# Four of six modulation groups of two layers made on VectorE, and fewer weight splits on GpSimd

## The chip, the core and the metric

The kernel runs on one core of a Trainium2 chip, as one program launched once. The metric is the device time of one execution in microseconds. TensorE multiplies matrices, VectorE and ScalarE do elementwise work, GpSimd does some more of it, and SyncE issues the DMAs. Each engine takes its own instructions in order and waits on semaphores for the others.

## The reference

Two blocks of two layers each run one after the other on `x` and a context, 256 tokens of 1024 features each. The first block's layers have a mixer of attention, Fourier and Hyena heads; the second's have a DeltaNet (layer 0) and a gated linear attention (layer 1). All four layers end in a feed-forward network (FFN). Each layer is steered by six vectors of 1024, made from a conditioning vector:

```
m = silu(c) @ w_mod + b_mod                        # 1024 -> 6 x 1024; c for x, c_ctx for the context
sh1, sc1, g1, sh2, sc2, g2 = split(m, 6)
x = x + g1 * mixer(rms_norm(x) * (1 + sc1) + sh1)
x = x + g2 * (relu(h @ w1) ** 2 @ w2),  h = rms_norm(x) * (1 + sc2) + sh2
```

In each block's second layer the context gives only keys and values, so it needs `sh1` and `sc1` alone: of groups 2 to 5 only the row of `c` is used there.

The DeltaNet has 8 heads of two value halves; each walks through four chunks of 128 tokens in both directions, its outputs are normalised per token and value half, multiplied by silu(z) (z is a projection of the layer's input, the gate), and multiplied by `w_out`.

## The kernel before

Activations lie feature by feature: a tile has 128 features in its partitions and the 512 tokens of both streams (`x` 0 to 255, context 256 to 511) in its columns. Every large matrix product is done in three passes on a reduced fp32 format. `weight` loads 512 KB of weights (`wr`), ScalarE rounds them to the high part `wh` (L307), and VectorE or GpSimd subtracts to get the low part `wl` (L308); this subtraction is called a split below. `mm3` issues the passes wh x rh, wh x rl, wl x rh (L316 to L318). For one tile of 128 output features and 1024 inputs that is 24 matmuls. GpSimd does the split where `pool=True` is passed (the first four weights of each FFN, two or so weights ahead of each next stage, some of the last mixer) and, by `pool_lo`, for the whole DeltaNet.

An FFN (`ffn`, `mlp`, `tail`) goes through four quarters. In each, the first matrix gives eight hidden tiles (24 matmuls each; then ScalarE's relu, VectorE's square at L610, ScalarE's L294 and VectorE's L295 for the two parts of it), and the second gives eight output tiles, added to `xs` at L659. FFN1 is that of the first block's layer 0, FFN2 that of the second block's layer 0; both have both streams, so n is 512.

The modulation vectors of all but the first layer's early groups are made in the background. `modulation` returns a list of steps, each a load of a few rows of 128 inputs (`wm`) and a piece of work. On TensorE (L394) the piece is 32 matmuls for four rows, which multiply silu(c) of both streams (`cvs`, 32 columns, two used) by 256 columns of weights, in four column strips of the array. The last piece of a group of 1024 outputs is followed, one step later, by `columns`: ScalarE's copy `ev`, four small matmuls (L405) that turn rows into columns, and the addition of the bias on VectorE (L406). `slot` is called after each tile of an FFN and starts a step each `every` slots; `quota` bounds the loads of a stage. The list runs in order: layer 1 of block 1, then both layers of block 2. The steps of block 1's layer 1 and part of block 2's fall into FFN1, later ones into FFN2; the tile `mod` of a layer is named `moda`, `modb` in the trace, and TensorE's output tile for it `pmd`.

The DeltaNet (`deltanet`) runs its heads in turn: `merge` and `steps` are long chains of small matmuls and VectorE operations, and between heads stand large products (`project`, `gates`, `write_out`) that fill TensorE meanwhile. `scale` normalises the outputs `ot` (the tiny operations are in `rsqrt`, L436 and L437), `readout` transposes them by eight matmuls (L452) and multiplies by the gates. For the last head nothing is left to project, so the generator `late` cuts the second gate and the output product of head 6 into 24 parts of three matmuls, which `between` puts into head 7's chains (16 of them at fixed places) while the rest follows after the last step. Then come `readout`, head 7's output product for stream `x` and then for the context, and behind each the norm for FFN2. SyncE's queue carries weights, `wm` loads and the DeltaNet's small transfers (`TT<-dout`) in program order.

Of the kernel before, what the change touches and what calls it, by code (L numbers as in the profile page):

```python
# [18 lines left out]
P = 128  # L19
# [15 lines left out]
def _moving(w):  # L35
    return _c(w.reshape(8, P, 6, 1024).transpose(2, 0, 1, 3))

# [92 lines left out]
def host_arrays(i):  # L130
# [5 lines left out]
    a["cv2"] = _c(np.stack([i["c_2"][0], i["c_ctx_2"]], 0).reshape(2, 8, P).transpose(2, 1, 0))  # L136
    for l in range(2):
# [67 lines left out]
class Net:  # L205
# [91 lines left out]
    def weight(self, src, into=None, pool=False, ahead=False):  # L297
# [22 lines left out]
    def lin(self, src, rhs, n0, n1, w=None, pool=False):  # L320
        w = w or self.weight(src, pool=pool)
        ps = self.mm_ps()
        self.mm3(ps[:, : n1 - n0], w, rhs, n0, n1)
        return ps[:, : n1 - n0]
# [42 lines left out]
    def modulation(self, wname, bname, cname, tag, batch=4, early=0):  # L367
# [47 lines left out]
        return mod, [s for cc in range(6) for s in steps(cc)]  # L415
# [103 lines left out]
    def follow(self, f, xs, S, gs, mod, shch, tag, win=None):  # L519
        f.update(h=self.rows16(), ws=None)  # L520

        def then(sv, y=None):
            if win and not f["ws"]:
                f["ws"] = [self.weight(w, pool=True, ahead=True) for w in win]
# [28 lines left out]
    def ffn(self, xs, g, w1, w2, mod, tag, streams, ys=None, h=None, quota=0, every=1, S=None, scales=None, before=None, then=None):  # L553
        one = len(streams) == 1
        with ExitStack() as st:
            self.pools(st, dict(n=(8, 256), h=3, acc=(4, 256), sq=(4, 256), rs=(1, 258)), dict(a=2, md=1, mm=5), 12 if one else 18, "a", quota)
# [4 lines left out]
            ws = [self.weight(self.a[w1][m], pool=True) for m in range(4)]  # L561
            self.background(1 if every == 2 else 0)
            self.load_ahead()
            self.every, self.slots = every, 0
# [5 lines left out]
            self.mlp(xs, h, ws, w1, w2, mod, 5, streams, S, scales or {"xc"[v]: 1.0 for (_, _, v) in streams}, before, then, nS)  # L570
# [4 lines left out]
    def mlp(self, xs, h, ws, w1, w2, mod, gch, streams, S, scales, before, then, nS):  # L575
        nc = self.nc
        n = 256 * len(streams)
        for s in range(4):
# [3 lines left out]
            for m in range(0, 8, 2):  # L582
# [13 lines left out]
                elif s == 0 and m == 0:  # L596
                    first = self.lins(ws[:4], h, streams)
# [73 lines left out]
    def pools(self, st, sb, ps, nr, pm, quota=0, pool_lo=False, nwm=2, wide=4, low=()):  # L671
        self.n += 1
        self.pool_lo = pool_lo
# [37 lines left out]
    def slot(self):  # L711
        self.slots += 1
        if self.slots % self.every == 0:
# [354 lines left out]
    def deltanet(self, xs, mod, h, ws, first):  # L1068
# [119 lines left out]
        def late(zs, og):  # L1188
            def use(ps):
                zs.append(ap.tile([P, 512], F32, tag="vf", bufs=2, name="z"))  # L1190
                nc.scalar.activation(zs[1], ps, AF.Silu)

            yield from self.lin_parts(lambda: self.weight(win[48]), h, 512, use)
# [124 lines left out]
        def merge(hd, c, parts):  # L1318
# [30 lines left out]
        def steps(hd, c, parts):  # L1349
# [4 lines left out]
            for step in range(4):  # L1354
                Sn = ap.tile([P, 512], F32, tag="S", bufs=2, name="S") if step < 3 else None
                for d in range(2):
# [31 lines left out]
                    self.between(parts, i.ins, 2 if step == 3 else 1)  # L1388
# [13 lines left out]
                S = Sn  # L1402
            return ot

        def scale(c, ot):
            ss = sp.tile([P, 4, 2], F32, tag="ss", name="ss")
            jk = junk()
            for ch in range(4):
                for v in range(2):
                    nc.scalar.activation(jk, ot[ch // 2][:, 256 * (ch % 2) + P * v : 256 * (ch % 2) + P * v + P], AF.Square,  # L1410
                                         accum_out=ss[:, ch, v : v + 1])
            nc.vector.scalar_tensor_tensor(ss, ss, 1.0 / 128, c["aq"].unsqueeze(2).to_broadcast([P, 4, 2]), ALU.mult, ALU.add)
            so = self.rsqrt(ss.rearrange("p c v -> p (c v)"), [P, 8], "o")
            for p in range(2):
                o = ot[p].rearrange("p (c i) -> p c i", i=P)
                nc.vector.tensor_tensor(o, o, so[:, 4 * p : 4 * p + 4].unsqueeze(2).to_broadcast([P, 4, P]), ALU.mult)
# [11 lines left out]
        def write_out(hd, og, S=None, then=None):  # L1428
            ws = [self.weight(a["dwout"][hd, mq]) for mq in range(2)]
            for sv in st if S else [(0, 512, 0)]:  # L1430
                for m in range(8):
                    c = slice(P * (m % 4), P * (m % 4) + P)
                    wh, wl = ws[m // 4]
                    ps = self.mm_ps()[:, : sv[1] - sv[0]]
                    self.mm3(ps, (wh[:, :, c], wl[:, :, c]), og, sv[0], sv[1])
                    if S:
                        self.finish(xs, m, ps, mod, 2, sv, S, dict(x=1.0, c=1.0))
                    else:
                        for s2 in st:
                            self.finish(xs, m, ps[:, s2[0] : s2[1]], mod, 2, s2, None, None)  # L1440
                if then:
                    then(sv)
# [5 lines left out]
        og, parts = None, iter(())  # L1448
        for hd in range(8):
            if hd == 7:  # L1450
                parts = late(zs, og)
            merge(hd, c, parts)
            ot = steps(hd, c, parts)
            if hd < 7:
                nxt = prepare(hd + 1, *proj)
            if 0 < hd < 7:
                write_out(hd - 1, og)
            if hd < 7:
                tokens(nxt)
# [4 lines left out]
            elif hd == 6:  # L1464
                zn = [gate(7, 0)]
            else:
                for part in parts:
                    part()
            with self.tc.issue_after(self.mark.ins):
                og = readout(ot, zs)  # L1470
            if hd < 6:
                zs = gates(hd + 1)
            elif hd == 6:
                zs = zn
            if hd < 7:
                c = nxt
# [4 lines left out]
        write_out(7, og, S, f["then"])  # L1481
# [4 lines left out]
    def gla(self, xs, mod, h, ws):  # L1486
# [46 lines left out]
        w3 = self.weight(win[2], [vtile().rearrange("p b n -> p (b n)").rearrange("p (k m) -> p k m", k=8).bitcast(F32R) for _ in range(2)], pool=True)  # L1533
# [5 lines left out]
        for m in range(4):  # L1539
            ps = self.lin(win[1 + m], h, 0, 512, w3 if m == 1 else None, True) if m else ps1  # L1540
# [6 lines left out]
        for m in range(4):  # L1547
            ps = self.lin(win[5 + m], h, 0, 256, None, m<3)
# [7 lines left out]
        def values(hd):  # L1556
            w = [self.weight(a["gwv"][hd, kh], pool=False) for kh in range(2)]
# [15 lines left out]
        def gate(hd):  # L1573
            zs = []
            for m in range(2):
                ps = self.lin(win[9 + 2 * hd + m], h, 0, 256, None, False)
# [146 lines left out]
    def run(self):  # L1723
# [8 lines left out]
        if not skip:  # L1732
            fng = None
            y = None
            for l in range(2):
                with ExitStack() as st:
# [5 lines left out]
                    self.pools(st, sb, ps, 7 if l else 10, "t", nwm=1, wide=3, low=("K", "V", "q", "PT", "E"))  # L1742
                    self.first_consts(st)
                    if l == 0:
# [4 lines left out]
                        mods = [self.modulation(f"wmod_{j}", f"bmod_{j}", "cv", f"a{j}", 4 if j else 3, 0 if j else 2) for j in range(2)]  # L1749
# [29 lines left out]
                        def early():  # L1779
                            self.background(2)  # L1780
                            ws = [self.weight(a["win_0"][m], pool=False) for m in (8, 9)]
                            self.background(5)
                            self.early = False
                            mods2.extend(self.modulation(f"amod_{j}", f"abmod_{j}", "cv2", f"b{j}") for j in range(2))
# [137 lines left out]
```

## Time and profile before

| what | value |
|---|---|
| time of three runs | 2652.54, 2655.13, 2656.1 us; median 2655.13 |
| the profiled execution | 2648.67 us |
| its span (first to last instruction) | 2646.9 us |
| mean granted TensorE clock | 0.977 of full speed |
| TensorE, VectorE, ScalarE, GpSimd busy | 95%, 62%, 43%, 14% of the span |

The span is the profiled execution without 1.8 us around it. A busy share is a mean over all stages, so what one stage is limited by is read from the windows of that stage. FFN1 lies between 328 and 694 us of the span, the DeltaNet's last head between about 1747 and 1853, FFN2 between 1866 and 2226. An instruction in the timeline has its start and its duration; the bracket behind it holds the idle time of its engine just before and what ended it.

### The profile page before, as it was taken

The numbers are of one execution on the slowest core, as the hardware profiler recorded it, in microseconds if no ns is written. First come the engines' busy times: TensorE is split into PE (matmuls) and PEld (weight loads), VectorE is DVE, ScalarE is ACT, GpSimd is POOL, SyncE is SP. The second block draws the span as 40 slices with busy tenths as digits, with TensorE's granted clock in tenths as the row PEclk, the third lists the DMA queues.
The fourth block names the chain that finished last, engine by engine and source line by source line (L and its number), as shares of the span: only waits on it lengthen the run. The fifth ranks groups of instructions, "written<-read, shape, count | busy, mean of one in ns | idle before, by whom it ended". The sixth has DMA issues, their size and how long they took to land. (4 is left out here: it accounts for less than half of the span.)

```text
span 2646.9 us, 40579 instructions
## 1 busy us (share of the span) xinstructions
PE 2503.5 (95%) x15740; PEld 2108.8 (80%) x15740; DVE 1648.9 (62%) x3449; ACT 1133.1 (43%) x2161; POOL 370.3 (14%) x268
## 2 busy tenths in 40 slices
PE   7999999999999999988999999977999999899999
PEld 4866877778886999867778877866877888698899
DVE  5555443333567777887877887767533435677676
ACT  3344333232355545663545444534422324564453
POOL 0000200000100100332333323312000001420100
PEclk8999999999999999999999999988999999999999
DMA  7334566663241466222122211211554522222554
GB/s 266 120 117 147 176 254 236 242 236 117 77 141 52 160 194 197 80 66 53 34 61 65 71 39 52 65 35 56 204 179 160 182 88 71 79 93 73 172 184 154
DMA packets 147105, 334.09 MB, mean 126 GB/s; under 512 B 57134, under 2 KB 68512, under 8 KB 146912
## 3 DMA queue, kind: packets, MB, share of 16 engines
q1 hardware_dynamic: 146656, 331.43, 38.6%
q8 instruction: 124, 2.03, 0.3%
q14 instruction: 69, 0.57, 0.1%
q0 software_dynamic: 256, 0.07, 0.0%
HBM read 327.78 MB, written 3.67 MB: 125 GB/s over the span
## 5 line engine op out<-in xcount | busy, mean ns | idle before, releaser
L307 ACT CAST wh<-wr 128x1024 fp32r<-128x1024 f32 (+1 forms) x421 | 426.1, 1016 | 700.2 <-PE pmm L317 511.4
L318 PE MATMUL pmm<-h,wl 128*128 128x512 f32 (+2 forms) x1800 | 624.6, 347 | 16.3 <-DVE wl L308 8.8
L316 PE MATMUL pmm<-h,wh 128*128 128x512 f32 (+2 forms) x1800 | 628.8, 349 | 6.9 <-ACT E L829 1.9
L317 PE MATMUL pmm<-h,wh 128*128 128x512 f32 (+2 forms) x1800 | 621.3, 345 | 0.0
L308 DVE TENSOR_TENSOR wl<-wr,wh 128x1024 fp32r<-128x1024 f32 (+1 forms) x333 | 392.3, 1180 | 288.8 <-ACT wh L307 282.3
L318 PE MATMUL pmm<-r,wl 128*128 128x256 f32 (+1 forms) x1312 | 444.3, 339 | 5.6 <-DVE wl L308 5.5
L316 PE MATMUL pmm<-r,wh 128*128 128x256 f32 (+1 forms) x1312 | 444.9, 340 | 4.5 <-DVE q L989 1.6
L317 PE MATMUL pmm<-r,wh 128*128 128x256 f32 (+1 forms) x1312 | 444.2, 339 | 0.1
L308 POOL TENSOR_TENSOR wl<-wr,wh 128x1024 fp32r<-128x1024 f32 x88 | 216.5, 2465 | 1383.1 <-ACT wh L307 724.4
L318 PEld LDWEIGHTS pmm<-h,wl 128*128 128x128 f32 x1800 | 346.6, 193 | 59.7 <-DVE wl L308 10.2
L316 PEld LDWEIGHTS pmm<-h,wh 128*128 128x128 f32 x1800 | 346.3, 192 | 53.0 <-issue 7.2
L317 PEld LDWEIGHTS pmm<-h,wh 128*128 128x128 f32 x1800 | 346.7, 193 | 37.1 <-issue 0.8
L316 PEld LDWEIGHTS pmm<-r,wh 128*128 128x128 f32 x1312 | 248.4, 190 | 38.7 <-issue 8.9
L318 PEld LDWEIGHTS pmm<-r,wl 128*128 128x128 f32 x1312 | 248.8, 190 | 32.0 <-DVE wl L308 7.0
L317 PEld LDWEIGHTS pmm<-r,wh 128*128 128x128 f32 x1312 | 249.1, 190 | 23.2 <-issue 1.7
L659 DVE SCALAR_TENSOR_TENSOR xs<-pmm,modb,xs 128x256 f32<-128x256 f32 x232 | 106.6, 477 | 133.0 <-PE pmm L318 133.0
L659 DVE SCALAR_TENSOR_TENSOR xs<-pmm,moda,xs 128x256 f32<-128x256 f32 x120 | 54.4, 480 | 146.7 <-PE pmm L318 146.5
L294 ACT CAST r<-h 128x256 fp32r<-128x256 f32 (+1 forms) x128 | 65.5, 513 | 126.8 <-DVE h L610 67.2
L295 DVE TENSOR_TENSOR r<-h,r 128x256 fp32r<-128x256 f32 (+1 forms) x128 | 72.9, 570 | 44.1 <-ACT r L294 40.7
L394 PE MATMUL pmd<-wm,cvs 128*32 128x256 f32 x1408 | 87.2, 382 | 0.0
L1371 ACT COPY e<-pa 128x256 f32<-128x256 f32 x64 | 23.8, 371 | 128.5 <-PE pa L1369 128.0
L394 PEld LDWEIGHTS pmd<-wm,cvs 128*32 128x32 f32 x1408 | 41.1, 109 | 40.1 <-issue 13.4
(484 smaller groups left out, 3834.7 us busy)
## 6 DMA issues: line engine op xcount, KB each, us to landing
wr<-w SPq DMA_DIRECT2D x128, 512.0 KB
wr<-f SPq DMA_DIRECT2D x128, 512.0 KB
wm<-amod SPq DMA_DIRECT2D x24, 2048.0 KB
wr<-dwin SPq DMA_DIRECT2D x49, 512.0 KB
wm<-wmod SPq DMA_DIRECT2D x12, 2048.0 KB
wr<-win SPq DMA_DIRECT2D x28, 512.0 KB
wm<-wmod SPq DMA_DIRECT2D x8, 1536.0 KB
wr<-gwin SPq DMA_DIRECT2D x17, 512.0 KB
```

Of the source, the lines that this page charges most:

```text
L294: self.nc.scalar.copy(hi, src)
L295: self.nc.vector.tensor_tensor(lo, src, hi.bitcast(F32), ALU.subtract)
L307: self.nc.scalar.copy(hi, raw)
L308: (self.nc.gpsimd if pool or self.pool_lo else self.nc.vector).tensor_tensor(lo, raw, hi.bitcast(F32), ALU.subtract)
L316: mm(ps, wh[:, k, :], rh[:, n0:n1], start=k == 0, stop=False)
L317: mm(ps, wh[:, k, :], rl[:, n0:n1], start=False, stop=False)
L318: self.mark = mm(ps, wl[:, k, :], rh[:, n0:n1], start=False, stop=k == last)
L394: self.last = nc.tensor.matmul(ps[32 * c : 32 * c + 32, :256], cs[:, k + i, :], raw[:, i, 256 * c : 256 * c + 256], start=k + i == 0, stop ...
L659: self.nc.vector.scalar_tensor_tensor(x, ps, mod[:, 8 * gch + m, v : v + 1], x, ALU.mult, ALU.add)
L1371: nc.scalar.copy(vA, ptr[:, :256])
```

## The change

Groups 2 to 5 of both second layers (`wmod_1`, `amod_1`) no longer go over TensorE. The host lays their weights out by output feature, 32 rows of [128 outputs, 1024 inputs] (`wmodr_1`, `amodr_1`), and c broadcast to 128 partitions (`cb`, `cb2`). A step loads up to three rows; VectorE multiplies each with silu(c) and sums it up in one instruction, and adds the bias. The context's columns of these groups are set to zero. TensorE's loads have three rows at most in place of four. A step is started each 1.5 slots in FFN1 and each 3 in FFN2, where it was 2 and 4.

The argument `pool` of `weight` is gone; GpSimd splits only in heads 1 to 5 of the DeltaNet. At the end of the DeltaNet both gates of head 7 are projected ahead of the readout of head 6, `late` has the output product of head 6 alone, its parts are put only into `merge` and into the first two of the four steps, the norm and the readout of head 7 are done per stream, the context first, and FFN2's first tiles begin with the context.

```diff
+def _rows(w):
+    return _c(w[:, 2048:].T.reshape(32, P, 1024))
...
-        (self.nc.gpsimd if pool or self.pool_lo else self.nc.vector).tensor_tensor(lo, raw, hi.bitcast(F32), ALU.subtract)
+        (self.nc.gpsimd if self.pool_lo else self.nc.vector).tensor_tensor(lo, raw, hi.bitcast(F32), ALU.subtract)
...
+        nc.gpsimd.memset(mod[:, 16:, 1], 0.0)
+        def rload(j, n):
+            raw = self.gp.tile([P, self.wide, 1024], F32, tag="wm", bufs=self.nwm, name="wm")
+            nc.sync.dma_start(raw[:, :n], self.a[rows][j : j + n].rearrange("k p n -> p k n"))
+            return raw
+        def rstep(j, n, raw):
+            m = mod[:, 16 + j : 16 + j + n, 0]
+            for i in range(n):
+                nc.vector.scalar_tensor_tensor(raw[:, i], raw[:, i], 1.0, self.cb, ALU.mult, ALU.mult, accum_out=m[:, i : i + 1])
+            nc.vector.tensor_tensor(m, m, self.small(bname)[:, 16 + j : 16 + j + n], ALU.add)
+        rs = [(lambda j=j, n=min(3, 32 - j): rload(j, n), lambda raw, j=j, n=min(3, 32 - j): rstep(j, n, raw)) for j in range(0, 32, 3)]
+        return mod, [s for cc in range(2) for s in steps(cc)] + rs
...
+            if cb:
+                self.cb = self.t("cb", 1024)
+                self.nc.sync.dma_start(self.cb, self.a[cb])
+                self.nc.scalar.activation(self.cb, self.cb, AF.Silu)
...
-        if self.slots % self.every == 0:
+        if self.slots >= self.every * (self.taken + 1):
+            self.taken += 1
...
-                    self.between(parts, i.ins, 2 if step == 3 else 1)
+                    if step < 2:
+                        self.between(parts, i.ins)
...
+                if step == 1 and half:
+                    half(ot)
...
+        parts = late(og)
+        merge(7, c, parts)
+        ot = steps(7, c, parts, lambda ot: scale(c, ot, (1,)))
+        scale(c, ot, (0,))
...
+        readout1(ot, zs, og, 1)
+        for part in parts:
+            part()
+        ws = [self.weight(a["dwout"][7, mq]) for mq in range(2)]
+        write_last(ws, og, st[1], S)
+        with self.tc.issue_after(self.mark.ins):
+            readout1(ot, zs, og, 0)
+        f["then"](st[1])
+        write_last(ws, og, st[0], S)
+        f["then"](st[0])
...
-                    self.ffn(xs, "g2_0", "w1_0", "w2_0", mods[0][0], "2_0", both, ys, None, 24, 2, S, None, before, lambda sv: f["then"](sv))
+                    self.ffn(xs, "g2_0", "w1_0", "w2_0", mods[0][0], "2_0", both, ys, None, 35, 1.5, S, None, before, lambda sv: f["then"](sv), cb="cb")
...
-        self.ffn(xs, "fg_0", "f1_0", "f2_0", mods2[0][0], "4", both, None, h, 12, 4, S, None, before, lambda sv: f["then"](sv))
+        self.ffn(xs, "fg_0", "f1_0", "f2_0", mods2[0][0], "4", both, None, h, 17, 3, S, None, before, lambda sv: f["then"](sv), [both[1], both[0]], "cb2")
```

VectorE in FFN1, where the first matrix of a quarter ends and the second begins (`h`, `r` are the hidden tiles and their low parts, `wl` a split, `xs` the sum). Before:

```order
L610 TENSOR_TENSOR h<-h,pmm 128x512
L295 TENSOR_TENSOR r<-h,r 128x512
L308 TENSOR_TENSOR wl<-wr,wh 128x1024
L610 TENSOR_TENSOR h<-h,pmm 128x512
L295 TENSOR_TENSOR r<-h,r 128x512
L308 TENSOR_TENSOR wl<-wr,wh 128x1024
L610 TENSOR_TENSOR h<-h,pmm 128x512
L406 TENSOR_TENSOR moda_118<-pmd,bmod_160 128x2x4x2
L308 TENSOR_TENSOR wl<-wr,wh 128x1024
L295 TENSOR_TENSOR r<-h,r 128x512
L308 TENSOR_TENSOR wl<-wr,wh 128x1024
```

and in the changed kernel:

```order
L316 TENSOR_TENSOR wl<-wr,wh 128x1024
L640 TENSOR_TENSOR h<-h,pmm 128x512
L437 SCALAR_TENSOR_TENSOR wm,moda_118<-wm,cb 128x1024
L303 TENSOR_TENSOR r<-h,r 128x512
L437 SCALAR_TENSOR_TENSOR wm,moda_118<-wm,cb 128x1024 x2
L316 TENSOR_TENSOR wl<-wr,wh 128x1024
L640 TENSOR_TENSOR h<-h,pmm 128x512
L438 TENSOR_TENSOR moda_118<-moda_118,bmod_161 128x3
L316 TENSOR_TENSOR wl<-wr,wh 128x1024
L303 TENSOR_TENSOR r<-h,r 128x512
L316 TENSOR_TENSOR wl<-wr,wh 128x1024
L689 SCALAR_TENSOR_TENSOR xs<-pmm,moda_117,xs 128x256 x2
```

A step's three sums and its small addition now stand among the last hidden tiles' squares and low parts.

TensorE at the end of the DeltaNet, the readout of head 7 (`pb<-k_id,ot`) and what stands around it. Before:

```order
L316 MATMUL pmm<-r,wh 128x512
L317 MATMUL pmm<-r,wh 128x512
L318 MATMUL pmm<-r,wl 128x512
L452 MATMUL pb<-k_id,ot 128x128 x8
L316 MATMUL pmm<-r,wh 128x256 x3
L317 MATMUL pmm<-r,wh 128x256
L318 MATMUL pmm<-r,wl 128x256
```

and in the changed kernel, where the readout comes in two halves (`pa` are products of the steps):

```order
L326 MATMUL pmm<-r,wl 128x512
L324 MATMUL pmm<-r,wh 128x512
L478 MATMUL pb<-k_id,ot 128x128 x4
L325 MATMUL pmm<-r,wh 128x512
L1395 MATMUL pa<-e,TT 128x128
L326 MATMUL pmm<-r,wl 128x512
L1395 MATMUL pa<-e,TT 128x128
L1411 MATMUL pa<-S,kq 128x256
...
L326 MATMUL pmm<-og,wl 128x256
L478 MATMUL pb<-k_id,ot 128x128 x4
L472 MATMUL pb<-ones,acc 128x1 x2
L324 MATMUL pmm<-og,wh 128x256 x3
```

The context's half moved up among the products of the last steps, and the other half stands behind the context's output product.

## Rows read from the trace of the kernel before

**Rows 1.** The page's first section: busy us, share of the span, instructions.
```profile
PE 2503.5 (95%) x15740; PEld 2108.8 (80%) x15740; DVE 1648.9 (62%) x3449; ACT 1133.1 (43%) x2161; POOL 370.3 (14%) x268
```

**Rows 2.** Windows: PE, PEld, DVE, ACT, POOL busy (instructions), PE clock, DMA share, GB/s.
```profile
328.00:694.00 366.00, 365.98 (x2196) 284.99 (x2196) 140.07 (x202) 105.85 (x146) 1.96 (x4) 1.00 0.58 205
...
1866.00:2226.00 360.00, 360.00 (x1959) 291.57 (x1957) 145.82 (x206) 106.78 (x145) 5.44 (x3) 1.00 0.47 161
...
340.00:350.00 10.00, 10.00 (x71) 7.39 (x70) 7.90 (x11) 5.29 (x9) 0.00 (x0) 1.00 0.97 358
```

**Rows 3.** Windows of FFN1 and FFN2, tile pmd alone: PE, PEld, DVE, ACT.
```profile
328.00:694.00 366.00, 50.55 (x784) 28.73 (x784) 2.03 (x12) 4.50 (x12) 1.00 0.58 205
1866.00:2226.00 360.00, 26.24 (x408) 14.84 (x408) 1.02 (x6) 2.23 (x6) 1.00 0.47 161
```

**Rows 4.** Timeline of TensorE in FFN1: start, duration in us, engine, line, operation.
```profile
404.89 0.39 PE L317 MATMUL pmm<-r,wh 128*128 128x512 f32 x1
405.12 0.39 PE L318 MATMUL pmm<-r,wl 128*128 128x512 f32 x1
405.43 1.93 PE L394 MATMUL pmd<-wm,cvs 128*32 128x256 f32 x32
407.30 0.50 PE L316 MATMUL pmm<-r,wh 128*128 128x512 f32 x1
...
418.08 0.39 PE L318 MATMUL pmm<-r,wl 128*128 128x512 f32 x1
418.31 0.51 PE L405 MATMUL pmd<-k_sel,ev 128*128 128x8 f32 x4
418.67 0.49 PE L316 MATMUL pmm<-h,wh 128*128 128x512 f32 x1
```

**Rows 5.** Timeline of VectorE in FFN1; in brackets the idle time before.
```profile
413.07 0.88 DVE L659 SCALAR_TENSOR_TENSOR xs<-pmm,moda,xs 128x256 f32<-128x256 f32 x2 [5.45 <-PE pmm L318]
413.93 1.23 DVE L308 TENSOR_TENSOR wl<-wr,wh 128x1024 fp32r<-128x1024 f32 x1
...
428.57 0.68 DVE L610 TENSOR_TENSOR h<-h,pmm 128x512 f32<-128x512 f32 x1
429.94 0.69 DVE L295 TENSOR_TENSOR r<-h,r 128x512 fp32r<-128x512 f32 x1 [0.69 <-ACT r L294]
```

**Rows 6.** Timeline of VectorE in the DeltaNet's preparation.
```profile
1107.19 0.68 DVE L1107 SCALAR_TENSOR_TENSOR g<-g 32x512 f32<-32x512 f32 x1 [1.88 <-ACT g L1106]
...
1122.22 0.69 DVE L1148 TENSOR_TENSOR g<-g 96x512 f32<-96x512 f32 x1
```

**Rows 7.** Timeline of GpSimd at the end of the DeltaNet.
```profile
1820.18 9.25 POOL L308 TENSOR_TENSOR wl<-wr,wh 128x1024 fp32r<-128x1024 f32 x4 [2.30 <-ACT wh L307]
```

**Rows 8.** Timeline of VectorE, the norm of head 7's outputs.
```profile
1819.48 0.17 DVE L436 TENSOR_TENSOR rst<-rsy 128x8 f32<-128x8 f32 x1
...
1824.88 2.27 DVE L437 TENSOR_TENSOR rst<-rst,rsh 128x8 f32<-128x8 f32 x1
```

**Rows 9.** Timeline of TensorE at the end of the DeltaNet.
```profile
1752.73 1.94 PE L452 MATMUL pb<-k_id,ot 128*128 128x128 f32 x8 [5.91 <-DVE ot L1416]
1758.26 2.05 PE L1333 MATMUL pa<-TT,Mt 128*128 128x128 f32 x8 [3.59 <-DMA TT<-dout]
...
1830.23 1.97 PE L452 MATMUL pb<-k_id,ot 128*128 128x128 f32 x8 [11.25 <-DVE ot L1416]
```

**Rows 10.** Windows: the end of the DeltaNet.
```profile
1746.80:1853.00 106.20, 74.46 (x429) 62.77 (x428) 68.13 (x158) 37.07 (x84) 19.45 (x9) 0.84 0.17 45
```

**Rows 11.** Chain of waits, where FFN2's first matmul stands: start, us, engine, tile.
```profile
1852.97 0.58 PE pmm L351
```

**Rows 12.** Waits of TensorE: us in all, count, longest.
```profile
PE pmm L318 <- POOL wl L308: 7.3, 2, 4.7
```

**Rows 13.** The page's fifth section, the splits: busy us, mean ns, idle before.
```profile
L308 DVE TENSOR_TENSOR wl<-wr,wh 128x1024 fp32r<-128x1024 f32 (+1 forms) x333 | 392.3, 1180 | 288.8 <-ACT wh L307 282.3
...
L308 POOL TENSOR_TENSOR wl<-wr,wh 128x1024 fp32r<-128x1024 f32 x88 | 216.5, 2465 | 1383.1 <-ACT wh L307 724.4
```

More of the change, by code (lines that the diff above doesn't have):

```diff
@@ L413, in steps @@
             return [(lambda k=k, n=n - k: load(k, n), lambda raw, k=k, n=n - k: step(k, n, raw)) for k, n in zip(ks, ks[1:])]
-        return mod, [s for cc in range(6) for s in steps(cc)]
+        if not rows:
+            return mod, [s for cc in range(6) for s in steps(cc)]
+        nc.gpsimd.memset(mod[:, 16:, 1], 0.0)
[10 more added lines that the diff above has]
+        return mod, [s for cc in range(2) for s in steps(cc)] + rs
     def gscale(self, mod, ch, gname, tag):
@@ L523, in then @@
             if win and not f["ws"]:
-                f["ws"] = [self.weight(w, pool=True, ahead=True) for w in win]
+                f["ws"] = [self.weight(w, ahead=True) for w in win]
             self.norm_one(f["h"], xs, sv, gs, mod, shch, y or self.stat_end(S, "xc"[sv[2]]), tag, True)
@@ L560, in ffn @@
             self.load_ahead(1)
-            ws = [self.weight(self.a[w1][m], pool=True) for m in range(4)]
-            self.background(1 if every == 2 else 0)
+            ws = [self.weight(self.a[w1][m]) for m in range(4)]
+            if cb:
+                self.cb = self.t("cb", 1024)
+                self.nc.sync.dma_start(self.cb, self.a[cb])
+                self.nc.scalar.activation(self.cb, self.cb, AF.Silu)
+            self.background(1 if every < 2 else 0)
             self.load_ahead()
-            self.every, self.slots = every, 0
+            self.every, self.slots, self.taken = every, 0, 0
             nS = None
@@ L596, in mlp @@
                 elif s == 0 and m == 0:
-                    first = self.lins(ws[:4], h, streams)
+                    first = self.lins(ws[:4], h, order)
                     pss = first[:2]
@@ L1185, in gates, with late @@
             return [gate(hd, 0), gate(hd, 1)]
[L1188 to L1193, printed above, removed]
+        def late(og):
             ws = [self.weight(a["dwout"][6, mq]) for mq in range(2)]
@@ L1346, in merge, with steps @@
                     nc.vector.tensor_tensor(mix(TT[1], 4 * hf, 4, s), v4(FT), v4(pzt), ALU.subtract)
-        def steps(hd, c, parts):
+        def steps(hd, c, parts=iter(()), half=None):
             kq, vt, D, mbt, ktm, TB = c["kq"], c["vt"], c["D"], c["mbt"], c["ktm"], c["TT"][1]
@@ L1447, in deltanet @@
         proj = project(1)
[L1448 to L1456, printed above, removed]
+        og = None
+        for hd in range(7):
+            self.pool_lo = 0 < hd < 6
+            merge(hd, c)
+            ot = steps(hd, c)
+            nxt = prepare(hd + 1, *proj)
+            if hd:
                 write_out(hd - 1, og)
-            if hd < 7:
-                tokens(nxt)
+            tokens(nxt)
             scale(c, ot)
@@ L1463, in deltanet @@
                 proj = project(hd + 2)
-            elif hd == 6:
-                zn = [gate(7, 0)]
-            else:
-                for part in parts:
-                    part()
+            else:
+                zn = gates(7)
             with self.tc.issue_after(self.mark.ins):
                 og = readout(ot, zs)
[L1471 to L1476, printed above, removed]
+            zs = gates(hd + 1) if hd < 6 else zn
+            c = nxt
+        parts = late(og)
+        merge(7, c, parts)
+        ot = steps(7, c, parts, lambda ot: scale(c, ot, (1,)))
+        scale(c, ot, (0,))
+        D = lambda: ap.tile([P, 4, P], F32, tag="D", bufs=8, name="og").rearrange("p s i -> p (s i)").bitcast(F32R)
+        og = [(D(), D()) for _ in range(2)]
         S = dict(acc={}, new=lambda n: ap.tile([P, 512], F32, tag="FT", bufs=2, name="acc")[:, :n],
@@ L1556, in values @@
         def values(hd):
-            w = [self.weight(a["gwv"][hd, kh], pool=False) for kh in range(2)]
+            w = [self.weight(a["gwv"][hd, kh]) for kh in range(2)]
             vs = vtile()
@@ L1821, in before @@
                             f["gs"] = gs
-                            f["ws"] = [self.weight(a["dwin"][m], pool=True, ahead=True) for m in range(2)]
+                            f["ws"] = [self.weight(a["dwin"][m], ahead=True) for m in range(2)]
                         if s == 3.5:
```

99 lines of the change are left out of this document (56 added, 43 removed).

## The prediction

> **What bounds the kernel now.** I read the page's first section, then the windows by stage, then the order in time of single engines in the stages that the change touches. TensorE is busy 95% of the span [rows 1], so only two things can shorten the run: less work for TensorE where it never waits, and less waiting where it does. The windows show the first kind: in the two-stream FFN of the first block (FFN1, 328 to 694 us) and of the second (FFN2, 1866 to 2226 us) TensorE is busy without a gap at full clock while VectorE is busy only 140 of 366 and 146 of 360 us [rows 2]. In just these stages it also makes the modulation vectors, 50.6 and 26.2 us of busy time [rows 3]. The second kind is the end of the DeltaNet mixer: between 1746.8 and 1853.0 us TensorE is busy 74.5 of 106.2 us and the mean granted clock is 0.84 [rows 10]. The order in time shows three long gaps there, 5.91 us before the readout of head 6, 3.59 us for a DMA, 11.25 us before the readout of head 7, and eight transposes after the third still take 1.97 us, at the lower of the two clocks [rows 9].
>
> **The change part by part.** A. Modulation taken off TensorE. Eight of the 24 groups go (four in FFN1, four in FFN2). One group costs TensorE two interruptions of 32 instructions and one of 4 small ones. In the stream, matmuls start 0.23 us apart; around a run of 32 the starts are 405.12 and 407.30, so it costs 2.18 - 0.23 = 1.95 us; around the run of 4 they are 418.08 and 418.67, so 0.36 us [rows 4]. A group is 2 x 1.95 + 0.36 = 4.26 us, eight are 34.1 us, all on the path, since nothing waits there [rows 2]. The ten groups that stay in these stages come in three loads and not two: one interruption more each, worth its overhead alone, 1.95 - 32 x 0.058 = 0.09 us (0.058 is 1.86 us over 32, the first start to the next stream's in [rows 4]), in all 0.9 us. A is -33.2 us.
>
> B. What VectorE takes over. It gets 64 multiply-and-sum instructions of 128x1024, in 11 steps of up to three per FFN, with one addition per step. The trace has none with the sum, so I bound it: a plain tensor_tensor of this shape takes 1.23 us [rows 5], and a scalar_tensor_tensor with both inputs in SBUF takes 0.68 us for 512 elements where a tensor_tensor takes 0.69 [rows 6], so from below 1.23; from above twice that, 2.46, if the sum needed a second pass. I take 1.3, near the rows. Is there room? A slot is 24 matmuls of 0.228 us = 5.47 us. In it VectorE does a residual pair and a split, 0.88 + 1.23 = 2.1 us, in the second matrix, or 0.68 + 0.69 + 1.23 = 2.6 us in the first [rows 5], on average 2.36. FFN1 starts a step every 1.5 slots, 8.2 us: 3 x 1.3 + 0.17 + 1.5 x 2.36 = 7.6 us, 93% of VectorE. FFN2 has 3 slots, 16.4 us, and needs 11.2. So it fits, tightly in FFN1. What the steps delay is the work queued behind them on VectorE: weights' low parts, which have four buffers (three slots, 16 us, of slack), and at the end of each first matrix the last hidden tile. That tile is needed when seven eighths of the next 24 matmuls are through, 4.8 us after the stream's end, and its chain of two ScalarE and two VectorE steps takes about 2.7 us; a step of up to 3.9 us in front of it can cost up to 1.8 us. Four such places fall among the steps: I put B at +4 us, with 0 and +32 as ends (the upper end is worked out under the rivals).
>
> A step also waits for its DMA, with all of VectorE's queue behind it. Per step 4.5 loads of 512 KB must land in 8.2 us, 288 GB/s. The trace has 358 GB/s at 0.97 of the DMA engines in one 10 us window of this stage, and a mean of 205 GB/s over it [rows 2]; so the rate exists, and I count no wait.
>
> A page of the Trainium skill speaks against this part: Vector Engine (DVE) Microarchitecture Reference, section "Points that are easy to get wrong", has it that a scalar_tensor_tensor with two SBUF sources that are not bf16 runs at half the rate. For the form without the sum the trace disagrees (0.68 against 0.69 us) [rows 6]; with the sum no row shows it. By the rule the forecast would be the first rival's time.
>
> C. The end of the DeltaNet mixer. Both gates of head 7 now stand before the readout of head 6: the second one's 24 matmuls (5.5 us) fill the gap of 5.91. The gap of 3.59 stays, as its DMA has the same place in SP's queue. The fillers in head 7's merges and steps go from 16 to 10 forced parts of 0.7 us; its chain is bound by latency, so that leaves some 2 us more of gaps there. The norm of head 7's outputs is split by stream. The context half runs among steps 2 and 3, and its 48 output matmuls, with the six parts that are left, about 10 us, stand where the 11.25 us gap was. The gap is also that long because four weight splits on GpSimd take 9.25 us from 1820.18 [rows 7] and hold VectorE's tiny operations of the norm, 2.27 us each in place of 0.17 [rows 8]; these splits go to VectorE, at 1.2 us each. Last, FFN2 starts with the context stream, whose norm is ready while the other stream's outputs are still made; before, its first matmul started at 1852.97 [rows 11]. Of 31.7 us idle [rows 10] I leave 0.5 + 3.6 + 9 in the merges and steps + 4 at the end = 17 and count 15 as won, and 5 us for the lower clock behind two gaps that go (the 1.97 us are twice what eight such transposes take at full clock, and some 5 us of matmuls after them run as slowly). C is -20 us; the ends are -9, the longest gap less one split's delay, and -27, if the new fillers hide nearly all.
>
> D. Other splits. Of 91 on GpSimd 51 move; 40 stay in heads 1 to 5. A split takes 2.47 us there and 1.18 on VectorE [rows 13], and while GpSimd runs one, VectorE's next operation with two SBUF inputs is held [rows 7, 8], so a split on GpSimd costs VectorE about what doing it does. TensorE waited 7.3 us for such splits directly [rows 12]. At DeltaNet's start and in head 0 VectorE is already the busiest engine beside TensorE, so some of it comes back as delay. I take -6, with ends -13 (the wait, and as much behind held operations) and +6 (five splits of 1.18 us on VectorE's path). The Silu of c, once in each FFN, sits among ScalarE's norm instructions, which run ahead of TensorE there: 0.
>
> Sum: -33.2 + 4 - 20 - 6 = -55.2. The profiled execution took 2648.67 us: 2593.5. The median of the runs shown, 2655.13, lies 6.5 above it, so I predict **2600 us**, and give all times below on that scale.
>
> **The rivals.** 1. VectorE is the bound in FFN1. At 2.46 us an instruction a step with its other work needs 7.4 + 0.17 + 3.5 = 11.1 us of the 8.2: 2.9 x 11 = 32 us in place of 4, time 2628; FFN2 still fits (14.6 of 16.4). For it: no row with the sum; against: [rows 6]. 2. The end of the mixer gives only its lower end, because the new fillers wait for weights or VectorE's queue: -9 for -20, time 2611. For it: 13 us of VectorE work lie between the last step and the readout of the second half. 3. DMA is the bound in FFN1: at 240 GB/s a step takes 9.8 us, 11 x 1.6 = 18 us, time 2618. Against: 358 GB/s in [rows 2]. 4. Slower than before: VectorE's sum is far dearer than the rows of its kin, and in order as it is it holds the hidden tiles and the weights. FFN1 then loses 11 x (3d + 3.7 - 8.2), FFN2 11 x (3d + 7.3 - 16.4); that eats the 59 us won elsewhere at d = 3.2 us, and at three times the plain operation, 3.7 us, FFN1 loses 73 and FFN2 22, time 2691. Against: every row of this engine at one element a cycle. 5. The change doesn't do what it says: the instructions in the orders are there, so no.
>
> **How the numbers follow.** Forecast 0.60 (its own range 2582 to 2612), rival 1 0.14, rival 2 0.12, rival 3 0.07, rival 4 0.05, no change 0.02. The range 2578 to 2630 takes in rivals 1 to 3, and leaves out rival 4 and a gain beyond -77. A measurement of this kernel tells 0.2%, about 5 us, from no change. Faster 0.93, same 0.02, slower 0.05.
>
> **What would show it.** In the profile after: in the same stages 512 and 136 modulation instructions in place of 784 and 408 [rows 3] (four groups of 68 fewer in each); FFN1 and FFN2 each shorter by 15 to 17 us with TensorE still without gaps; the new VectorE instructions near 1.3 us; no gap over 4 us before the readout of head 7; VectorE's tiny operations there near 0.17 us. Gaps of TensorE on hidden tiles or weights in FFN1, with VectorE near 100% busy, would make rival 1 right; with VectorE waiting for wm loads, rival 3.

## The result and the profile after

The changed kernel takes 2585.75 us (median of four runs, 2584.5 to 2593.28) against 2653.84 before: a ratio of 0.9749, interval 0.9728 to 0.9769, so 61 to 72 us less. The forecast was 2600, 55 us less, with a range of 2578 to 2630. The profiled execution took 2585.91 us, its span 2584.1. The table has the starts of the same matmuls in both traces, as lengths of stages, and beside them what the steps A to D foresaw. FFN2's first matmul before is the one at 1852.15 us; the row at 1852.97 in [rows 11] is its fourth.

| stage (us) | before | after | difference | foreseen |
|---|---|---|---|---|
| up to FFN1's first matmul | 310.3 | 315.5 | +5.2 | 0 |
| FFN1, to the next layer's first | 410.6 | 394.5 | -16.1 | A, B: -15 to -17 |
| that layer and its FFN | 358.0 | 358.0 | +0.1 | 0 |
| DeltaNet, to the readout of head 0 | 187.0 | 169.4 | -17.6 | part of D (-6) |
| to the readout of head 5 | 411.0 | 414.7 | +3.7 | part of D |
| to FFN2's first matmul | 175.3 | 158.4 | -16.9 | C: -20 |
| FFN2, to the last layer's first | 383.3 | 366.7 | -16.6 | A, B: -15 to -17 |
| the last layer | 411.5 | 406.9 | -4.6 | part of D |

The page's first section after, which answers to [rows 1]: VectorE has taken 64 sums and 51 more splits, and GpSimd has lost 135 us of its 370.

```profile
PE 2463.6 (95%) x15196; PEld 2082.7 (81%) x15196; DVE 1721.3 (67%) x3659; ACT 1133.8 (44%) x2157; POOL 235.2 (9%) x217
```

The windows of FFN1 and FFN2, as long as those of [rows 2], and the densest stretch of sums in FFN1 (columns as there).

```profile
317.00:683.00 366.00, 364.42 (x2044) 288.76 (x2044) 180.82 (x284) 108.19 (x155) 4.61 (x7) 1.00 0.61 213
...
1812.00:2172.00 360.00, 9.16 (x136) 4.74 (x136) 0.34 (x2) 0.74 (x2) 0.99 0.49 162
...
365.00:441.00 76.00, 75.83 (x347) 61.63 (x346) 68.02 (x122) 21.20 (x27) 0.31 (x1) 1.00 0.85 319
```

The middle row is that of the tile pmd in FFN2, which answers to [rows 3]: 136 modulation instructions where 408 stood (in FFN1 520 where 784 stood and 512 were foreseen). In the densest 76 us VectorE is busy 68 us, 90%, and DMA moves 319 GB/s, yet TensorE is busy 75.8 of 76. The group of the new instruction in the list of instructions by line, kept apart by shape (count, busy us, mean ns, idle before):

```profile
L437 DVE SCALAR_TENSOR_TENSOR wm<-wm,cb 128x1024 f32<-128x1024 f32 x64 | 76.4, 1220 | 4.2 <-DMA wm<-amodr 2.4 <-DMA wm<-wmodr 1.8
```

1.22 us with the sum, as long as the plain tensor_tensor of the shape (1.23 in [rows 5]); a read of the sum of 0.08 us follows each. The rule of the Trainium skill (Vector Engine (DVE) Microarchitecture Reference, "Points that are easy to get wrong") that this form with two sources in SBUF that are not bf16 runs at half the rate is not borne out here.

The end of the DeltaNet after: the window that answers to [rows 10], and what TensorE waited for from the readout of head 5 on (us in all, count, longest).

```profile
1721.80:1810.54 88.74, 67.16 (x410) 57.44 (x408) 64.64 (x172) 36.03 (x90) 3.21 (x4) 0.91 0.20 53
```
```profile
PE pmm L358 <- DVE xs L689: 6.8, 1, 6.8
PE pa L1359 <- DMA TT<-dout: 4.1, 1, 4.1
PE pb L478 <- DVE ot L1448: 4.1, 1, 4.1
```

Of 31.7 us idle [rows 10] 21.6 are left. The gaps before the two readouts (5.91 and 11.25 us in [rows 9]) have become one of 4.1; a new one of 6.8 us stands before FFN2's first matmul, which needs the context's norm. A tiny operation of the norm, 2.27 us in [rows 8], on VectorE:

```profile
1789.60 0.16 DVE L463 TENSOR_TENSOR rst<-rst,rsh 128x4 f32<-128x4 f32 x1
```

All this looks like the prediction come true, and nearly every sign that it named is there. None of those signs can tell its term C from its term D. The experiments show that two of its four terms were right only in their sum.

### The profile page after: what moved, and what is told of

Its sections match the earlier page's. It is cut to its first block, busy times and chain, and to the rows that moved or that the text cites. A ratio compares the mean times of both kernels' runs of the same rounds, so it can differ in the third digit from the quotient of the medians.

```text
span 2584.1 us, 39685 instructions
## 1 busy us (share of the span) xinstructions
PE 2463.6 (95%) x15196; PEld 2082.7 (81%) x15196; DVE 1721.3 (67%) x3659; ACT 1133.8 (44%) x2157; POOL 235.2 (9%) x217
## 4 chain that ended last, share of the span: by engine, by line
PE 77%; DVE 10%; issue 5%; ACT 3%; DMA 3%; POOL 1%; SPq 0%; DVEq 0%; ACTq 0%; POOLq 0%
PE pmm L324 19%; PE pmm L326 18%; PE pmm L325 18%; PE pmd L402 2%; DVE wl L316 1%; DMA wm<-wmod 1%; PE ps L1035 1%; ACT wh L315 1%; PE pmm L359 1%; PE pa L1395 1%; PE pa L1371 1%; PE pmm L358 1%; PE pmm L360 1%; PE pa L1413 1%; PE pa L1366 1%
## 5 line engine op out<-in xcount | busy, mean ns | idle before, releaser
L316 DVE TENSOR_TENSOR wl<-wr,wh 128x1024 fp32r<-128x1024 f32 (+1 forms) x381 | 448.6, 1179 | 275.9 <-ACT wh L315 269.2
L326 PE MATMUL pmm<-r,wl 128*128 128x256 f32 (+1 forms) x1280 | 435.0, 341 | 2.6 <-DVE wl L316 2.5
L324 PE MATMUL pmm<-r,wh 128*128 128x256 f32 (+1 forms) x1280 | 435.4, 341 | 1.9 <-DVE q L1020 1.4
L325 PE MATMUL pmm<-r,wh 128*128 128x256 f32 (+1 forms) x1280 | 433.8, 339 | 0.0
L324 PEld LDWEIGHTS pmm<-h,wh 128*128 128x128 f32 x1800 | 342.2, 190 | 56.8 <-issue 6.7
L325 PEld LDWEIGHTS pmm<-h,wh 128*128 128x128 f32 x1800 | 342.5, 190 | 39.5 <-issue 0.8
L324 PEld LDWEIGHTS pmm<-r,wh 128*128 128x128 f32 x1280 | 241.3, 189 | 33.8 <-issue 7.6
L326 PEld LDWEIGHTS pmm<-r,wl 128*128 128x128 f32 x1280 | 241.6, 189 | 28.9 <-DVE wl L316 4.7
L325 PEld LDWEIGHTS pmm<-r,wh 128*128 128x128 f32 x1280 | 241.8, 189 | 23.2 <-issue 1.7
L542 POOL TENSOR_TENSOR h<-n,h 128x256 fp32r<-128x256 f32 x28 | 21.4, 764 | 1218.9 <-ACT h L541 1218.5
L316 POOL TENSOR_TENSOR wl<-wr,wh 128x1024 fp32r<-128x1024 f32 x40 | 96.2, 2406 | 146.8 <-ACT wh L315 112.9
L437 DVE SCALAR_TENSOR_TENSOR wm<-wm,cb 128x1024 f32<-128x1024 f32 x64 | 76.4, 1220 | 4.2 <-DMA wm<-amodr 2.4
```

Of the source, the lines that this page charges most:

```text
L316: (self.nc.gpsimd if self.pool_lo else self.nc.vector).tensor_tensor(lo, raw, hi.bitcast(F32), ALU.subtract)
L324: mm(ps, wh[:, k, :], rh[:, n0:n1], start=k == 0, stop=False)
L325: mm(ps, wh[:, k, :], rl[:, n0:n1], start=False, stop=False)
L326: self.mark = mm(ps, wl[:, k, :], rh[:, n0:n1], start=False, stop=k == last)
L437: nc.vector.scalar_tensor_tensor(raw[:, i], raw[:, i], 1.0, self.cb, ALU.mult, ALU.mult, accum_out=m[:, i : i + 1])
```

## The experiments

Each ratio is to the kernel before, in runs on the same chip; microseconds of a ratio are worked out with 2653. Stages and windows are those of the one profiled execution of each kernel. Where two new kernels are compared by their medians, they can come from different chips; the kernel before has medians of 2651.6 to 2654.0 us on these.

**The parts alone.** Three kernels take one part each from the change to the kernel before. The first has the rows of weights, the three-row loads and the pacing.

> The kernel before with the modulation part alone (groups 2 to 5 of both second layers as row sums on VectorE, three-row loads, the new pacing); DeltaNet end and splits as before. Theory: the rows cost TensorE nothing and save what the change's two stages showed, 11 us up to the end of FFN1 and 16.6 us in FFN2: 28 us less than before, near 2626 us. Rival (the sums hold the hidden tiles back where GpSimd no longer helps, so alone they are worth more): 33 us or more less. Rival (half of it is lost again at the stage ends): at most 18 us less.

2620.95 us, ratio 0.9881 (0.9866 to 0.9896): 28 to 36 us less. FFN1 takes 393.3 us in place of 410.6, FFN2 365.4 in place of 383.3, and the stretch before FFN1 has lost the same 5 us. The theory holds, though its sum was 3 us short and the interval does not exclude the 33 us of the first rival.

The second has the DeltaNet's end.

```diff
+        parts = late(og)                  # output product of head 6 alone
+        merge(7, c, parts)
+        ot = steps(7, c, parts, lambda ot: scale(c, ot, (1,)))
...
+        write_last(ws, og, st[1], S)      # context first
```

> The kernel before with the new end of the DeltaNet alone (both gates early, norm and readout by stream, context first in FFN2); modulation on TensorE and GpSimd's splits as before. Theory: the reordering itself wins the gap of 5.9 us and part of the 11.25, but the splits on GpSimd at the end still hold VectorE's tiny operations: 9 to 14 us less than before, 2640 to 2645. Rival (the reordering is all of it): 20 us less, 2634. Rival (nothing without the splits moved): within 4 us of before.

2655.92 us, ratio 1.0012 (1.0004 to 1.0021): 1 to 6 us slower. All but the third expectation fall. From the readout of head 5 to FFN2 it wins 5.9 us (169.4 for 175.3), and each of heads 1 to 5 takes 86.9 us where it took 86.1, 3.7 us together; FFN2 takes 1.9 us more. With the splits on GpSimd the norm in two halves has its waits as before. Rows of VectorE in the norm's second half, whose readout TensorE waits 8.1 us for, and of GpSimd beside them, in this kernel:

```profile
1824.75 2.30 DVE L1443 SCALAR_TENSOR_TENSOR ss<-ss,aq 128x4 f32<-128x4 f32 x1
1827.36 2.01 DVE L458 TENSOR_SCALAR rsy<-ss 128x4 int32<-128x4 int32 x1
```
```profile
1819.79 9.56 POOL L316 TENSOR_TENSOR wl<-wr,wh 128x1024 fp32r<-128x1024 f32 x4 [18.59 <-ACT wh L315]
```

The third has the splits: `pool` ignored, and `self.pool_lo = 0 < hd < 6` in the old loop over the heads.

> The kernel before with the splits alone moved: GpSimd splits only in heads 1 to 5 of the DeltaNet. Theory from the two traces: 14 us less in the DeltaNet's start and head 0, 4 to 5 us less in the last mixer, 2 to 6 us less at the DeltaNet's end, together 20 to 25 us less, near 2632. Rival (my prediction's term D): 6 us less, 2648. Rival (gain at the start is only a shift that the later heads swallow): under 4 us.

2614.52 us, ratio 0.9859 (0.9843 to 0.9874): 33 to 42 us less, more than any theory said. The start to the readout of head 0 takes 171.1 us (187.0), the readout of head 5 to FFN2 163.0 (175.3), the last layer 405.0 (411.5). So the longest gap before a readout shrinks from 11.25 to 6.3 us with no reordering at all. The page's first section of this kernel:

```profile
PE 2487.8 (95%) x15740; PEld 2099.5 (80%) x15740; DVE 1649.5 (63%) x3500; ACT 1136.6 (44%) x2163; POOL 237.8 (9%) x217
```

VectorE does 51 splits more, 60 us at 1.18 us each [rows 13], and is busy 0.6 us more than before [rows 1]. The three parts add up: -32, +3, -37 are -66, the change is -67. To see whether the new end pays beside the other two, it was left out: the first and the third kernel's edits together.

> The kernel before with the modulation part and the moved splits, and the old end of the DeltaNet. Theory after the first runs (rows -31, splits -37, the reordered end nothing by itself): 2583 to 2588 us, the same as the changed kernel within 0.2%. Rival (the reordered end pays once the splits are off GpSimd, as the prediction's term C has it): 2595 us or more, 10 us above the changed kernel.

2585.01 us, ratio 0.9747 (0.9734 to 0.976), the changed kernel's 0.9749. The theory holds; term C is worth nothing that shows.

**Why the splits were worth 37 us.** First the start of the DeltaNet alone goes back to GpSimd, in the changed kernel:

```diff
+            self.pool_lo = True          # from the DeltaNet's start
-            self.pool_lo = 0 < hd < 6
+            self.pool_lo = hd < 6
```

> The changed kernel with the splits of the DeltaNet's start and head 0 (13 of 128x1024) on GpSimd again; heads 1 to 5 as they are, heads 6 and 7 on VectorE. Theory: the first readout comes 14 to 16 us later, nothing else changes: 2600 us. Rival (prediction's D: such splits cost VectorE about what doing them does): within 5 us of the changed kernel.

2601.51 us, ratio 0.9805 (0.9791 to 0.9818), 16 us over the changed kernel. The theory holds; in the trace 15 splits have gone back to GpSimd, not 13. Next VectorE keeps these splits and GpSimd repeats each of them for nobody:

```diff
+        if getattr(self, 'dup', False):
+            for q in range(4):
+                self.nc.gpsimd.tensor_tensor(self.dn.tile([P, 2, P], F32, tag="dup", bufs=1, name="dup"), raw[:, 2 * q : 2 * q + 2], hi[:, 2 * q : 2 * q + 2].bitcast(F32), ALU.subtract)
```

> The changed kernel, VectorE doing all splits of the DeltaNet's start and head 0 as it does, and GpSimd doing each of them a second time in four pieces of 128x256 into a spare tile that nobody reads. Theory (GpSimd's reads hold VectorE's operations with two SBUF inputs, so a split there costs even if nobody waits for it): 8 to 16 us more than the changed kernel, in the start and head 0. Rival (a split on GpSimd costs only by its own 2.5 us for the one who waits): within 3 us, apart from what later raw tiles cost.

2599.45 us, ratio 0.98 (0.9787 to 0.9813), 14 us over the changed kernel: useless work on GpSimd costs about what moving the splits there costs. The windows from the DeltaNet's first matmul to the readout of head 0, one row for a kernel: before, after, this one.

```profile
1078.87:1265.87 187.00, 162.23 (x897) 134.40 (x897) 149.20 (x327) 94.93 (x205) 63.47 (x36) 0.94 0.22 59
```
```profile
1068.05:1237.49 169.44, 155.00 (x897) 129.12 (x897) 144.75 (x342) 97.48 (x207) 26.96 (x21) 0.97 0.24 65
```
```profile
1069.98:1254.17 184.19, 160.53 (x896) 132.53 (x896) 153.58 (x342) 97.87 (x207) 86.55 (x81) 0.94 0.23 60
```

VectorE is the third busy time in a row and GpSimd the fifth; the granted clock follows. From before to after VectorE has 15 instructions more, 18 us of splits, and is busy 4.5 us less; with the duplicates it has the same 342 and is busy 8.8 us more. But this run holds more than one effect: ScalarE also waited 10.9 us for the duplicates to release weight buffers, and 14.8 us of stage are not 8.8. TensorE's part of these rows shows two pieces: 5.5 of the 14.8 us are longer busy time for the same matmuls, at a granted clock of 0.94 in place of 0.97, and 9.2 are idle time. From before to after it is 7.2 us of busy time, at the same two clocks, and 10.3 of idle time. How the idle time divides between held operations and late weights stays open.

In heads 1 to 5 the same question goes the other way: no split on GpSimd at all (`self.pool_lo = False` in the changed kernel).

> The changed kernel with the 40 splits of heads 1 to 5 on VectorE too, none on GpSimd. A head takes 86.9 us, TensorE is busy about 83 of them, VectorE about 69 with GpSimd's 29 beside it. Theory (what GpSimd holds up is about what the split costs on VectorE): VectorE's busy time per head stays within 4 us, and the time within 5 us of the changed kernel. Rival 1 (VectorE becomes the bound, 8 more splits of 1.2 us a head on its chain): 10 to 40 us more. Rival 2 (as at the start, every split off GpSimd pays): 5 to 15 us less.

2572.28 us, ratio 0.97 (0.9686 to 0.9713), 13 us below the changed kernel; the second rival holds. One head of the changed kernel, and the same head of this one:

```profile
1391.42:1478.34 86.92, 83.21 (x486) 69.06 (x485) 69.00 (x165) 41.72 (x105) 28.30 (x16) 1.00 0.22 57
```
```profile
1386.52:1470.19 83.67, 82.16 (x486) 69.77 (x484) 69.98 (x172) 41.82 (x106) 9.27 (x8) 1.00 0.24 60
```

Seven splits more on VectorE, 8.5 us, make it 1 us busier. The 13 us lie in the four heads from the readout of head 1 to that of head 5 (334.4 us for 347.6); up to the readout of head 1 nothing is won (237.2 us from the DeltaNet's start, for 236.6). The last step takes GpSimd's other two-input operations out of the DeltaNet (`Mt` and every second product with `D` go to `nc.vector`).

> The kernel of the run without splits on GpSimd (2572 us), with the DeltaNet's other two-input operations of GpSimd on VectorE as well (per head four of 128x256 and two of 128x512, 5.9 us of GpSimd a head). Theory (GpSimd holds VectorE for about as long as VectorE would need itself): within 5 us of that run, VectorE's busy time per head within 2 us. Rival (these stand on the chain of a head's preparation, and VectorE has 70 of 83.5 us already): 5 to 20 us more. Rival (still pays): 5 us less or better.

2558.12 us, ratio 0.9642 (0.9629 to 0.9655): 14 us less again, the last rival. One operation of VectorE shows the hold by itself, the product `Mt<-Mt,g`; its group before, after, and in this kernel:

```profile
L1255 DVE TENSOR_TENSOR Mt<-Mt,g 128x256 f32<-128x256 f32 x32 | 28.0, 876 | 6.8 <-POOL Mt L1254 6.8
```
```profile
L1281 DVE TENSOR_TENSOR Mt<-Mt,g 128x256 f32<-128x256 f32 x32 | 23.8, 742 | 6.2 <-POOL Mt L1280 6.1
```
```profile
L1281 DVE TENSOR_TENSOR Mt<-Mt,g 128x256 f32<-128x256 f32 x32 | 13.4, 418 | 0.3
```

The same work takes 876, 742 and 418 ns on average, as GpSimd has more or less to do beside it. The Trainium skill (SBUF — State Buffer, "SBUF: two separate sides") says that VectorE's operations with two SBUF inputs and GpSimd's that read SBUF exclude each other through a shared pair of ports, for a whole instruction. The trace agrees: 2.27 us for a tiny operation beside a split of 2.3 us [rows 7, 8], 0.17 without. In these traces an operation with one tensor input can be held too: the L458 shown above, in the kernel with the new end alone, takes 2.01 us beside GpSimd, and 0.16 in the changed kernel.

**How much room VectorE has.** In the changed kernel each sum is done twice, the second into a spare column (`accum_out=self.ndg[:, i : i + 1]`).

> The changed kernel with each of the 64 multiply-and-sum instructions issued twice (the second sum goes to a spare column and is not used). It adds 39 us of VectorE in 75 us of FFN1, where VectorE is busy about 80% now, and 39 us in some 90 us of FFN2. Theory (VectorE bounds when its work exceeds the time of the slots, as in the first rival of the prediction): 10 to 30 us more than the changed kernel, nearly all of it in FFN1, FFN2 unchanged. Rival (buffers of weights and hidden tiles take the delay up, steps only slide later): within 3 us of the changed kernel.

2608.15 us, ratio 0.983 (0.9811 to 0.9849), 22 us over the changed kernel by the medians; the profiled run lies at the fast end of its four, 13 us over. Windows of this kernel: FFN1, the dense stretch in it, FFN2.

```profile
315.40:726.51 411.11, 397.01 (x2236) 316.62 (x2233) 233.26 (x395) 120.42 (x180) 7.05 (x10) 0.99 0.56 195
365.00:480.00 115.00, 103.21 (x445) 82.15 (x444) 112.69 (x193) 31.17 (x40) 0.31 (x1) 0.96 0.67 233
1826.84:2193.74 366.90, 365.90 (x1857) 305.65 (x1857) 234.68 (x399) 116.87 (x169) 5.45 (x15) 0.99 0.48 159
```

FFN1 is 16.6 us longer, with VectorE busy 112.7 of 115 us in its dense stretch; TensorE waited 11.4 us for splits there. FFN2 has room and takes the same 367 us. So the theory holds: another 39 us of VectorE are more than FFN1 has room for.

Groups 0 and 1 of both second layers were then moved to VectorE too, on the kernel without splits on GpSimd. The columns for the context take a second sum a row.

```diff
+                if both:
+                    stt(self.jk, raw[:, i], 1.0, self.dcb, ALU.mult, ALU.mult, accum_out=mod[:, j + i : j + i + 1, 1])
```

> The kernel without splits on GpSimd (2572 us), with groups 0 and 1 of both second layers on VectorE too, once with c and once with the context's c: 32 more sums of 1.22 us in each FFN, steps of one or two rows, modulation on TensorE left only for the two first layers. Theory (rows cost TensorE nothing while VectorE fits in the slots): four groups of 4.26 us less, 17 us, 2555. Rival (in FFN1 the steps of one row, 2.4 us of sums a slot of 5.5 beside 2.4 us of other work, hold hidden tiles and weights): 10 us of it is lost again, 2565 or more.

2572.49 us, ratio 0.969 (0.9677 to 0.9704), against 0.97 without: nothing, where 17 us were looked for. FFN1 takes 397.2 us and FFN2 372.1, 2.7 and 5.4 us more than in the changed kernel although TensorE has less to do. VectorE's wait in FFN2 for the context's c:

```profile
DVE jk L440 <- ACT dcb L601: 9.9, 1, 9.9
```

A sum that waits 9.9 us holds the splits queued behind it; TensorE waits 4.3 us for ScalarE's part of a hidden tile and 3.5 us for a split in this FFN, and the clock granted in it falls from 0.99 to 0.97. In FFN1 there is no such wait. There VectorE is busy 77.0 of the 83 us from 317 on, and TensorE waits 3.4 us for a hidden tile and 2.3 for a split, which is what the rival describes. So in FFN2 the order of the loads spoilt the idea, and in FFN1 VectorE was too full; whether the other groups can pay in a better order stays open.

**A kernel faster than both.** Without the reordered end, and with no split on GpSimd:

> The kernel before with the modulation part and no split on GpSimd at all, and the old end of the DeltaNet: the run of 2572 us without the reordered end. Theory (the reordered end is worth nothing): within 5 us of 2572. Rival (it pays once VectorE is free of GpSimd everywhere): 2580 or more. Rival (it costs 0.8 us in each of heads 1 to 5): 2567 to 2569.

2566.21 us, ratio 0.9674 (0.9661 to 0.9688), 6 us below the run with it; neither rival's number, nearest to the last. The two intervals just touch and the two profiled executions lie the other way round (2571.87 and 2569.96 us), so this difference is at the edge of what the runs tell. And with the other operations off GpSimd as well:

> The kernel before with the modulation part, the old end of the DeltaNet, and in the DeltaNet no split and no two-input operation on GpSimd: the run of 2558 us without the reordered end. Theory (the two effects add: the old end was worth 6 us without splits on GpSimd): 2551 to 2554 us. Rival (what the old end won came from waits on GpSimd's other operations, gone there): 2558, no change.

2557.2 us, ratio 0.9651 (0.9634 to 0.9668), the same as with the reordered end (0.9642). The rival's number holds; no run shows its reason. By the ratios the two are 26 and 28 us faster than the changed kernel.

## Why the prediction came out

**A was right.** -33.2 was foreseen, -29.2 with B; the part alone gives 28 to 36 us. FFN1 and FFN2 are 32.6 us shorter in the changed kernel and 35.1 with the part alone, but one of their modulation steps has only moved: it stood behind FFN1's first matmuls and now stands ahead of them, outside the stage, at the lower of the clock's two levels. Before and after:

```profile
313.16 1.93 PE L394 MATMUL pmd<-wm,cvs 128*32 128x256 f32 x32
```
```profile
312.75 2.79 PE L402 MATMUL pmd<-wm,cvs 128*32 128x256 f32 x24
```

With 1.95 us for it the two FFNs have won 30.7 us, and 33.2 with the part alone. Of the 5.2 us lost ahead of FFN1, which were not foreseen, 2.7 are this step. The rest can be scatter: the kernel with the new end alone, where modulation is as before, also reaches FFN1 3.1 us later.

**B was right in its terms, and its cost was nothing.** 1.3 us an instruction were taken, 1.22 and a read of 0.08 were measured; 93% of VectorE were foreseen in the dense stretch, 90% are there. The +4 us for delayed hidden tiles did not come: TensorE waited 0.2 us for VectorE's splits in all FFN1 and for no hidden tile. The first rival priced twice the work at 32 us for 4; with twice the work FFN1 lost 16.6. Four buffers of weights, and DMA at 319 GB/s, were enough, so the third rival falls too.

**C failed.** -20 was foreseen, with ends -9 and -27; alone the new end gives +3 us, beside the other parts 0. The failed step is the sentence that the gaps of 5.91 and 11.25 us are won by matmuls put in their places. The matmuls stand there, and the gap moved. With the splits moved, the two readouts wait 10.0 us in the old order and 4.1 in the new, and FFN2's first matmul waits 1.0 and 6.8: some 11 us either way. These are the waits of the old order, in the kernel without the new end; those of the new one stand in the section on the result.

```profile
PE pb L477 <- DVE ot L1446: 10.0, 2, 6.2
PE pmm L357 <- ACT h L540: 1.0, 1, 1.0
```

Most of the 16.9 us that this end lost came from the splits, which alone shorten it by 12.3 us. Four pairs of kernels here differ in the order of the end alone. In them the new order wins 5.9 to 7.2 us from the readout of head 5 to FFN2, less than the lower end of the forecast; of the 7.2, beside the moved splits, 4.0 are TensorE's busy time at a granted clock of 0.95 in place of 0.92. It gives back 1.6 to 3.7 us in heads 1 to 5, 0.3 to 2.1 in FFN2 and 0.9 to 2.0 in the last layer, costs that the prediction does not have. The trace of before had the cause of the long gap: [rows 7] and [rows 8] stand in the working, but as one split's delay in a term about order.

**D failed in its size.** -6 was foreseen, with ends -13 and +6; the splits alone give -33 to -42. Its premise, that a split on GpSimd costs VectorE about what doing it does, is borne out: 51 splits more, 0.6 us more busy. The conclusion was wrong. It counted VectorE's time as equal and so the gain as small; but a held operation stands on the chain that TensorE waits for, and the split itself takes 2.47 us in place of 1.18 [rows 13] before its weight can be used. How much each of the two is worth no run separates, and a part of the gain goes with the granted clock, which D did not count. The bound from below, the waits put down to GpSimd and as much again [rows 12], could not hold it, since a held operation is listed as VectorE's own busy time and the wait for it as a wait for VectorE.

So -26 for C and D together met -34 by two errors of opposite sign; the total says nothing on either.

## What to carry to other kernels

Where two engines exclude each other, price work on the second by what it adds to the first: compare the mean duration of one operation of the same shape in stretches where the other engine is idle and where it is busy, here 0.17 and 2.27 us. A gap before a readout is first to be looked for in the engine that the readout waits for; filling the gap with other work helps only when that engine is late for a reason that the filler doesn't share. A total that comes out is no evidence for its terms: each part alone, and the whole without one part, are what told them apart here.

## What was not expected of the hardware

Moving 40 splits, 48.8 us of VectorE at 1.22 us each, off GpSimd raised VectorE's whole busy time from 1721.3 to 1726.9 us. In the DeltaNet's heads 1 to 5 the kernels with the reordered end take 0.8 us more a head (86.9 for 86.1) with the same TensorE instructions in the same order; TensorE's busy time has the difference (83.2 for 82.4). It sits in the products that read `h`. In the heads their matmuls start 0.232 to 0.233 us apart in all eight kernels with the new end and 0.227 in all six with the old: after, 28 of them follow one another from 1717.82 to 1724.35 us, before, 46 from 1677.99 to 1688.43. There are 672 from the readout of head 0 to that of head 5, so some 0.0055 us each makes up the 3.7 us. The products that read `r` in FFN1 and FFN2 keep 0.227 in every kernel. What in the new end slows these matmuls no run tells.
